# The first tile's modulation weights and first weights, laid out in memory in the order of their fetch

## The chip, the core and the metric

The kernel runs on one core of one Trainium2 chip. The metric is the device time of one execution in microseconds, as the median of several; three runs of the kernel before took 755.28 to 755.37, median 755.32. Five engines with their own instruction streams work side by side: TensorE (matrix products; PE, its weight loads PEld), VectorE (DVE), ScalarE (ACT), GpSimd (POOL) and SyncE (SP). In this kernel SP issues nearly all transfers from HBM, the chip's main memory, into the on-chip memory; sixteen DMA engines carry them out. An instruction waits until the transfer that it needs has landed on all of these.

## The reference

One decoder layer over 512 positions of width 1024 in fp32: two attention branches (forgetting and stick-breaking) fed by one input projection, a gated merge, a layer norm, a gated MLP with a short convolution, a second layer norm. Before each of the two sublayers a conditioning vector `c` scales and shifts the input:

```python
mod = c @ w_ada + b_ada
sh1, sc1, gt1, sh2, sc2, gt2 = [m[:, None, :] for m in jnp.split(mod, N_MOD, axis=-1)]
u = x * (1.0 + sc1) + sh1
proj = u @ w_in
```

So nothing of the projection can start before a part of `mod` is known: `sh1` and `sc1` for the rows of `w_in` that are to be used first. Each element of `mod` is an inner product of 1024 terms.

## The kernel before

**Tiles.** The width of 1024 is cut into eight tiles of 128 (`KT`), one channel to a partition. For tile `j` the kernel needs 128 rows of shift weights and 128 rows of scale weights (each row the 1024 weights of one element of `mod`), 128 rows of the input projection's first 904 columns with six bias values ahead of them (`w1`, 910 columns in all), and 128 rows of the transposed input (`xT`, 512 positions).

**Head.** At the start TensorE runs a few products with zeros (`zeros`), then four products that copy `c` to all partitions, a quarter of 256 columns into each of four PSUM banks (`grp[4]` to `grp[7]`), then more products with zeros. They don't use the modulation weights.

**Loading.** `first_load(j)` takes two tiles `wa` of 128x1024 (index 0 shift, index 1 scale), one `raw` for the first weights and one `xt`. For `j` above 0 these are four transfers. For `j` 0 they are cut finer: the weights come in halves of 512 columns, first half of shift, first half of scale, second half of shift, second half of scale, 256 KB each; then columns 0 to 389 of `w1`, then `xt`, then columns 390 to 909. All of these are issued by SP, in the order written (SP's order is set by hand). In HBM a row of `wa0` has 4096 bytes and one of `w1` 3640, so each of these cut transfers takes a part of every row. The transfers use eight completion semaphores in turn, so the ninth issue waits for the landing of the first.

**The first tile.** `first_zero` forms the inner products of tile 0, quarter by quarter as the broadcast of `c` is cut: for quarter `q` VectorE multiplies 256 columns of shift weights, then of scale weights, with `cq`, and sums along the row; the sum goes to `modr[:, w, 0, q]`, with `w` 0 for shift and 2 for scale. GpSimd adds up the partial sums of quarters 0 to 2, and the bias from the first columns of `raw`; VectorE adds the last quarter, which gives `modc`. ScalarE copies the quarters of `c` on for later use, splits the first 384 columns of the weights in two parts (`hi_of`; VectorE's `lo_of` makes the second), and applies scale and shift to `xt`, giving `uh`. Each fp32 product on TensorE is made of three products with such split operands. The block runs under `chain["on"]`, which keeps each engine's instructions in the order in which they are written.

**The tiles after it.** For `j` 1 to 7 `first_acc` makes the inner products with one VectorE instruction over 1024 columns each (line 216), `first_split` splits the weights, `first_mod` applies them, and `first_mm` adds 24 products per tile into eight banks (line 330). Two tiles are loaded ahead; five buffers stand for `wa`, four for `raw`. Where `chain` is off, the order on VectorE, ScalarE, GpSimd and TensorE is chosen by a planner with its own durations for instructions and transfers, within the dependencies and the orders given by hand (`issue_after`).

Lines of the profile: 227 to 230 are the loads of tile 0; 233 to 235 those of the others; 67 and 70 stand for every instruction recorded under `chain`; 100 and 103 are `hi_of` and `lo_of`.

Of the kernel before, what the change touches and what calls it, by code (L numbers as in the profile page):

```python
# [12 lines left out]
ALU = mybir.AluOpType  # L13
# [3 lines left out]
P = 128  # L17
T = 512
D = 1024
KT = D // P  # L20
# [8 lines left out]
W1B = W1C + 6  # L29
# [19 lines left out]
def layer_kernel(ctx: ExitStack, tc: tile.TileContext, out, xT, x, crow, wa0, wa1, w1, wct, wv, bf,  # L49
                 wp, wo, lncol, lnrow, wup, cwb, wdn):  # L50
    nc = tc.nc
# [23 lines left out]
    V, S, PE, G = Pinned(nc.vector), Pinned(nc.scalar), Pinned(nc.tensor), Pinned(nc.gpsimd)  # L75
# [54 lines left out]
    modr = const([P, 6, KT, 4], F32, "modr")  # L130
# [88 lines left out]
    def first_load(j):  # L219
        wa = [early.tile([P, D], F32, name=nm("wa"), tag="wa", bufs=5) for _ in range(2)]  # L220
        r = stg.tile([P, 1024], F32, name=nm("raw"), tag="raw", bufs=LOADS)
        xt = z(F32, "xt")
        if j == 0:
            for e in range(2):
                c = slice(e * 512, (e + 1) * 512)
                for q in range(2):
                    nc.sync.dma_start(wa[q][:, c], wa0[j, q][:, c])
            nc.sync.dma_start(r[:, 0:390], w1[j][:, 0:390])
            nc.sync.dma_start(xt, xT[j * P : (j + 1) * P, :])
            nc.sync.dma_start(r[:, 390:W1B], w1[j][:, 390:W1B])  # L230
        else:
            for q in range(2):
                nc.sync.dma_start(wa[q], wa0[j, q])
            nc.sync.dma_start(r[:, 0:W1B], w1[j])
            nc.sync.dma_start(xt, xT[j * P : (j + 1) * P, :])
        if j == 1:
            nc.sync.dma_start(bfs, bf)
        pend[j] = [wa, xt, r]
# [4 lines left out]
    def first_zero():  # L243
        wa, xt, r = pend[0]
        h, l = first_wide()
        for q in range(4):
            c = slice(q * 256, (q + 1) * 256)
            cq = grp[4 + q][:, 0:256]
            for w, t in zip((0, 2), wa):
                V.scalar_tensor_tensor(t[:, c], t[:, c], 1.0, cq, ALU.mult, ALU.mult, accum_out=modr[:, w, 0, q : q + 1])  # L250
            part = [modr[:, w, 0, :] for w in (0, 2)]
            if q == 0:
                G.tensor_scalar_add(part[1][:, 0:1], part[1][:, 0:1], 1.0)
            for w, m in zip((0, 2), part):
                if q in (1, 2):
                    G.tensor_tensor(m[:, 0:1], m[:, 0:1], m[:, q : q + 1], ALU.add)
                if q == 3:
                    V.tensor_tensor(modc[:, w, 0:1], m[:, 0:1], m[:, 3:4], ALU.add)
            for w, m in zip((0, 2), part):
                if q == 2:  # L260
                    G.tensor_tensor(m[:, 0:1], m[:, 0:1], r[:, w : w + 1], ALU.add)
            if q < 3:
                S.activation(cbc[:, c], cq, AF.Copy)
# [4 lines left out]
        r = r[:, 6:W1B]  # L268
# [501 lines left out]
    for p in (5, 6, 7):  # L770
        add_pair(p)
        for _ in range(3):
            if bj:
                j = bj.pop(0)
# [262 lines left out]
    for n in range(NSPLIT):  # L1037
        wt = weights(wui[n], 1 if n + 1 < NSPLIT else 0)
# [5 lines left out]
    for n in range(2 * FT):  # L1044
# [10 lines left out]
        t = z(F32, "cv")  # L1055
# [19 lines left out]
    for i in range(2):  # L1075
        t = fin.tile([P, D], F32, name=f"ln2_{i}", tag=f"ln2_{i}")
# [12 lines left out]
    for j in range(FT - LATE):  # L1089
        w = weights(wdi[j])  # L1090
# [4 lines left out]
    for i in range(NB):  # L1095
        tb = slice(i * P, (i + 1) * P)
        r = x1[i]
# [5 lines left out]
        for n, (e, c0, c1) in enumerate(pieces):  # L1103
            sole = (i, e) == own
            ps = bank()[:, 0 : c1 - c0] if sole else acc[i][e]
            for q in range(LATE):
                w = [ws[q][a][e][:, c0:c1] for a in range(2)]
# [19 lines left out]
def _pack(inputs):  # L1127
# [3 lines left out]
    c = np.ascontiguousarray  # L1131
    w_in, w_ada = a["w_in"], a["w_ada"]
    r = {}
# [1 line left out]
    r["x"] = a["x"][0]  # L1135
    r["crow"] = a["c"]
    wt = c(w_ada.T).reshape(6, KT, P, D)
    r["wa0"] = c(wt[0:2].transpose(1, 0, 2, 3))
    r["wa1"] = c(wt[2:6].reshape(4 * KT, P, D))
    bm = a["b_ada"].reshape(6, KT, P)  # L1140
    bcol = bm[[0, 3, 1, 4, 2, 5]].transpose(1, 2, 0).reshape(D, 6)
# [5 lines left out]

    first = [w_in[:, s : s + P] for s in (col("q", 0), col("k", 0), col("q", 1))]
    cols = np.concatenate([bcol] + first + [w_in[:, 2568:3080], w_in[:, 1536:1544]], axis=1)
    r["w1"] = c(cols.reshape(KT, P, W1B))  # L1150
    r["wv"] = c(w_in[:, 1024:1536].reshape(4, 2, P, 512).transpose(0, 2, 1, 3).reshape(4, P, D))
    starts = [col(*t) for t in TILES]
    r["wct"] = c(np.stack([w_in[:, s : s + P].reshape(KT, P, P).transpose(1, 0, 2).reshape(P, D) for s in starts]))
# [35 lines left out]
```

## Time and profile before

| | |
|---|---|
| median of three runs | 755.32 us (755.28 to 755.37) |
| the profiled execution's own time | 755.47 us |
| its span, first to last instruction | 753.3 us |
| TensorE busy | 741.5 us, 98% of the span |
| VectorE / ScalarE / GpSimd busy | 546.6 / 351.6 / 127.2 us |
| granted TensorE clock, mean | 0.998 |
| first product that uses loaded weights | 9.65 us |
| bytes moved | 100.46 MB, mean 133 GB/s |

A row of the timeline or of the chain of waits begins with the start in us and the duration in us, then the engine and the line; in brackets behind it stand the engine's idle time just before and what ended it. Rows of a group of instructions give a count (x4), busy time and mean. A row of the DMA issues gives what is written from what, the issuing engine's queue (SPq), how many issues, KB of each, and the median time from issue to landing. A row of windows gives, for a stretch of time, its length and then the busy time and count for PE, PEld, DVE, ACT and POOL, the granted clock, the DMA engines' share and GB/s.

### The profile page before, as it was taken

What the parts mean: (1) busy time and instruction counts of PE and PEld (TensorE: products, weight loads), DVE (VectorE), ACT (ScalarE), POOL (GpSimd) and SP (SyncE); (2) the same over time, 40 slices, a digit from 0 to 9 for tenths busy, and PEclk for the clock granted to TensorE, in tenths of its full rate; (3) what the DMA queues carried; (4) which work ended last, traced back from release to release, by engine and by line L of the source; (5) the groups of instructions that cost most, each with busy time, mean ns of one, the idle gap of its engine ahead of it and who ended that gap; (6) DMA issues with size and microseconds to landing.
All of it is one profiled execution on the core that took longest, in us unless ns stands there. A gap on an engine that the chain in (4) does not pass through costs nothing.

```text
span 753.3 us, 9519 instructions
## 1 busy us (share of the span) xinstructions
PE 741.5 (98%) x3502; PEld 620.8 (82%) x3502; DVE 546.6 (73%) x896; ACT 351.6 (47%) x587; POOL 127.2 (17%) x153
## 2 busy tenths in 40 slices
PE   8999999999999999999999999999999999999995
PEld 6878888888888888888898888888888888888885
DVE  6888989867688875596987887666755686333666
ACT  4568868368656654343246334444444442212300
POOL 3103000021110000000000690000000136455400
PEclk9999999999999999999999999999999999999999
DMA  8941332434334434564234424433333234324111
GB/s 328 405 164 56 113 120 105 141 99 153 103 114 136 154 112 167 169 232 164 86 112 140 157 98 137 134 118 125 127 115 109 85 110 150 103 85 140 56 40 73
DMA packets 31376, 100.46 MB, mean 133 GB/s; under 512 B 4145, under 2 KB 4673, under 8 KB 31330
## 3 DMA queue, kind: packets, MB, share of 16 engines
q1 hardware_dynamic: 29824, 97.69, 37.7%
q0 software_dynamic: 1504, 2.17, 1.1%
q8 instruction: 27, 0.44, 0.2%
q14 instruction: 19, 0.16, 0.1%
q10 hardware_dynamic: 2, 0.00, 0.0%
HBM read 96.63 MB, written 2.11 MB: 131 GB/s over the span
## 4 chain that ended last, share of the span: by engine, by line
PE 97%; DVE 1%; DMA 1%; ACT 0%; SPq 0%; issue 0%; DVEq 0%
PE ps L140 56%; PE ps L330 5%; PE ps L1085 5%; PE ps L1084 5%; PE ps L1086 5%; PE ps L613 3%; PE ps L70 2%; PE ps L585 2%; PE ps L794 2%; PE ps L796 2%; PE ps L795 2%; PE ps L523 1%; PE ps L522 1%; PE ps L496 1%; PE ps L497 1%; PE ps L498 1%
## 5 line engine op out<-in xcount | busy, mean ns | idle before, releaser
L103 DVE TENSOR_TENSOR wl<-raw,wh 128x1024 fp32r<-128x1024 f32 (+1 forms) x99 | 133.0, 1345 | 55.0 <-ACT wh L100 54.9
L140 PE MATMUL ps<-u2h,wh 128*128 128x512 f32 (+1 forms) x376 | 141.2, 376 | 0.0
L140 PE MATMUL ps<-u2l,wh 128*128 128x512 f32 (+1 forms) x376 | 141.0, 376 | 0.0
L140 PE MATMUL ps<-u2h,wl 128*128 128x512 f32 (+1 forms) x376 | 133.5, 375 | 0.0
L100 ACT ACTIVATE wh<-raw 128x1024 fp32r<-128x1024 f32 (+1 forms) x99 | 103.5, 1048 | 61.5 <-PE ps L1086 46.2
L140 PE MATMUL ps<-uh,wh 128*128 128x512 f32 x213 | 84.1, 395 | 0.0
L140 PE MATMUL ps<-ul,wh 128*128 128x512 f32 x213 | 83.3, 391 | 0.0
L140 PEld LDWEIGHTS ps<-u2h,wh 128*128 128x128 f32 x376 | 70.8, 188 | 13.0
L140 PEld LDWEIGHTS ps<-u2l,wh 128*128 128x128 f32 x376 | 70.8, 188 | 12.8
L140 PEld LDWEIGHTS ps<-u2h,wl 128*128 128x128 f32 x376 | 70.3, 188 | 12.6
L140 PE MATMUL ps<-uh,wl 128*128 128x512 f32 x213 | 78.9, 390 | 0.0
L683 POOL TENSOR_TENSOR raw<-raw,gt 128x1024 f32<-128x1024 f32 x22 | 56.4, 2568 | 92.8 <-DVE cv L1057 42.9
L1057 DVE SCALAR_TENSOR_TENSOR cv<-ps,cw,cv 128x511 f32<-128x511 f32 x44 | 32.9, 748 | 52.6 <-ACT cv L1056 52.6
L1056 ACT ACTIVATE cv<-ps,cw 128x512 f32<-128x512 f32 x44 | 34.1, 775 | 44.6 <-PE ps L140 44.6
L1084 PE MATMUL ps<-wh,hh 128*128 128x512 f32 x128 | 49.8, 389 | 0.0
L1085 PE MATMUL ps<-wl,hh 128*128 128x512 f32 x128 | 49.8, 389 | 0.0
L1086 PE MATMUL ps<-wh,hl 128*128 128x512 f32 x128 | 49.8, 389 | 0.0
L140 PEld LDWEIGHTS ps<-uh,wl 128*128 128x128 f32 x213 | 40.0, 188 | 8.7
L140 PEld LDWEIGHTS ps<-uh,wh 128*128 128x128 f32 x213 | 40.0, 188 | 8.0
L140 PEld LDWEIGHTS ps<-ul,wh 128*128 128x128 f32 x213 | 40.1, 188 | 7.8
L100 ACT ACTIVATE hh<-cv 128x512 fp32r<-128x512 f32 x22 | 13.9, 632 | 58.2 <-DVE cv L1064 58.2
L216 DVE SCALAR_TENSOR_TENSOR ada<-ada,cbc 128x1024 f32<-128x1024 f32 x24 | 29.2, 1218 | 8.7 <-DMA ada<-in_wa 8.6
(245 smaller groups left out, 1429.8 us busy)
## 6 DMA issues: line engine op xcount, KB each, us to landing
raw<-in_wup SPq DMA_DIRECT2D x44, 512.0 KB, 3.4
raw<-in_wct SPq DMA_DIRECT2D x29, 512.0 KB, 3.7
ada<-in_wa SPq DMA_DIRECT2D x24, 512.0 KB, 4.4
raw<-in_wdn SPq DMA_DIRECT2D x22, 512.0 KB, 3.3
wa<-in_wa SPq DMA_DIRECT2D x14, 512.0 KB, 7.4
raw<-in_wp SPq DMA_DIRECT2D x8, 512.0 KB, 3.3
raw<-in_wo SPq DMA_DIRECT2D x8, 512.0 KB, 3.4
raw<-in_wa SPq DMA_DIRECT2D x8, 512.0 KB, 3.3
```

The source lines that it names most:

```text
L100: S.activation(o, i, AF.Copy, scale=scale)
L103: return V.tensor_tensor(o, i, fl(hi), ALU.subtract)
L140: PE.matmul(ps, w, u, start=first and n == 0, stop=last and n == 2)
L216: V.scalar_tensor_tensor(wt, wt, 1.0, cbc, ALU.mult, ALU.mult, accum_out=raw)
L330: PE.matmul(grp[g], w, u, start=j == 0 and n == 0, stop=j == KT - 1 and n == (1 if g == 7 else 2))
L613: PE.matmul(ps[:, to : to + w], v_part(br, h, j), src[e][:, so : so + w], start=a == 0 and j == 0, stop=a == 1 and j == 3)
L683: G.tensor_tensor(r, r, gt[1], ALU.mult)
L1056: S.activation(t, ps, AF.Identity, bias=cw[:, n, 3:4], scale=cw[:, n, 2:3])
L1057: V.scalar_tensor_tensor(t[:, 1:], ps[:, 0:511], cw[:, n, 1:2], t[:, 1:], ALU.mult, ALU.add)
L1084: PE.matmul(ps, hh[j][:, tb], w[0], start=first, stop=False)
L1085: PE.matmul(ps, hh[j][:, tb], w[1], start=False, stop=False)
L1086: PE.matmul(ps, hl[j][:, tb], w[0], start=False, stop=last)
```

## The change

Three things change, all for tile 0 alone.

In the packing of the inputs on the host the two 512 KB blocks of `wa0[0]` are cut anew: the first block now holds, for each of the 128 rows, columns 0 to 511 of the shift weights and behind them columns 0 to 511 of the scale weights; the second block holds columns 512 to 1023 of both. `w1[0]` becomes flat: all rows' first 390 columns one after another, then all rows' remaining 520 columns.

In `first_load` two transfers of 512 KB, in rows of 4096 bytes, take the place of the four of 256 KB in rows of 2048; the two transfers of first weights read one contiguous stretch each, in rows of 1560 and 2080 bytes as before.

In `first_zero` the operand of each product is looked up in the new place: quarter `q` lies in `wa[q // 2]`, shift at 0 and scale at 512 columns, each with 256 columns for the quarter. The number of products, their sizes and their order stay.

```diff
         if j == 0:
-            for e in range(2):
-                c = slice(e * 512, (e + 1) * 512)
-                for q in range(2):
-                    nc.sync.dma_start(wa[q][:, c], wa0[j, q][:, c])
-            nc.sync.dma_start(r[:, 0:390], w1[j][:, 0:390])
+            flat = w1[j].rearrange("p c -> (p c)")
+            for q in range(2):
+                nc.sync.dma_start(wa[q], wa0[j, q])
+            nc.sync.dma_start(r[:, 0:390], flat[0 : P * 390].rearrange("(p c) -> p c", c=390))
             nc.sync.dma_start(xt, xT[j * P : (j + 1) * P, :])
-            nc.sync.dma_start(r[:, 390:W1B], w1[j][:, 390:W1B])
+            nc.sync.dma_start(r[:, 390:W1B], flat[P * 390 : P * W1B].rearrange("(p c) -> p c", c=W1B - 390))
...
-            for w, t in zip((0, 2), wa):
-                V.scalar_tensor_tensor(t[:, c], t[:, c], 1.0, cq, ALU.mult, ALU.mult, accum_out=modr[:, w, 0, q : q + 1])
+            for k, w in enumerate((0, 2)):
+                t = wa[q // 2][:, k * 512 + (q % 2) * 256 : k * 512 + (q % 2) * 256 + 256]
+                V.scalar_tensor_tensor(t, t, 1.0, cq, ALU.mult, ALU.mult, accum_out=modr[:, w, 0, q : q + 1])
...
-    r["wa0"] = c(wt[0:2].transpose(1, 0, 2, 3))
+    wa0 = c(wt[0:2].transpose(1, 0, 2, 3))
+    wa0[0] = wa0[0].reshape(2, P, 2, 512).transpose(2, 1, 0, 3).reshape(2, P, D)
+    r["wa0"] = wa0
...
-    r["w1"] = c(cols.reshape(KT, P, W1B))
+    w1 = c(cols.reshape(KT, P, W1B))
+    w1[0] = np.concatenate([w1[0, :, 0:390].ravel(), w1[0, :, 390:].ravel()]).reshape(P, W1B)
+    r["w1"] = w1
```

## The prediction

> **What bounds the kernel now.** First I read the busy shares and the shares of the chain of waits that ended last, from the profile's page.
>
> ```profile
> PE 741.5 (98%) x3502; PEld 620.8 (82%) x3502; DVE 546.6 (73%) x896; ACT 351.6 (47%) x587; POOL 127.2 (17%) x153
> PE 97%; DVE 1%; DMA 1%; ACT 0%; SPq 0%; issue 0%; DVEq 0%
> ```
>
> TensorE is busy nearly throughout, so what starts it late costs its full length. Where that start is late, the same chain in order of time (0 to 60 us) tells:
>
> ```profile
> 2.12 5.23 DMA wa<-in_wa
> 7.38 0.83 DVE wa L70 x5
> ...
> 8.59 0.17 DVE modc L70
> 8.79 0.82 ACT uh L70
> 9.65 41.15 PE ps L330 x179
> ```
>
> The only transfer in the chain is the fourth quarter of the first modulation weights. It is issued at 2.12, lands 5.23 later, at 7.35, and VectorE, ScalarE and TensorE follow in turn until the first real matmul at 9.65. From there to 50.80 the chain is TensorE alone, and the DMA's 1% of it is used up by these 5.23 us (0.7% of 753.3). So microseconds saved before 9.65 are kept as long as nothing new is late behind it.
>
> VectorE's rows of the head (timeline, 3.5 to 8.8) show who waits for which quarter:
>
> ```profile
> 3.56 0.42 DVE L67 SCALAR_TENSOR_TENSOR wa<-wa,ps 128x256 f32<-128x256 f32 x1 [1.09 <-PE ps L70]
> 4.95 0.42 DVE L70 SCALAR_TENSOR_TENSOR wa<-wa,ps 128x256 f32<-128x256 f32 x1 [0.96 <-DMA wa<-in_wa]
> ...
> 6.78 0.42 DVE L70 SCALAR_TENSOR_TENSOR wa<-wa,ps 128x256 f32<-128x256 f32 x1 [0.71 <-DMA wa<-in_wa]
> 7.38 0.42 DVE L70 SCALAR_TENSOR_TENSOR wa<-wa,ps 128x256 f32<-128x256 f32 x1 [0.17 <-DMA wa<-in_wa]
> 8.40 0.35 DVE L70 TENSOR_TENSOR modc<-modr 128x1 f32<-128x1 f32 x2
> ```
>
> Eight products (three and four stand in the gap), one every 0.34 us when nothing is missing: from 7.38 three of them to 8.40. The three waits that lie between them are all for transfers. After the last landing there are three products left, then the two additions that give `modc`.
>
> **The old transfers.** SP issues four of 256 KB, 0.47 apart; the view of DMA issues, asked for one issue at a time, gives 2.7, 3.7 and 5.0 us to landing for the first three:
>
> ```profile
> 0.73 1.82 SPq L227 DMA_DIRECT2D wa<-in_wa  x4
> wa<-in_wa SPq DMA_DIRECT2D x1, 256.0 KB, 2.7
> wa<-in_wa SPq DMA_DIRECT2D x1, 256.0 KB, 3.7
> wa<-in_wa SPq DMA_DIRECT2D x1, 256.0 KB, 5.0
> ```
>
> So the megabyte is in 6.62 us after its first issue (7.35 less 0.73). **The new transfers** are two of 512 KB with 4096-byte rows. This profile has such pairs on an idle queue, later in the kernel. Issue rows, then their times to landing (view of DMA issues over each single issue):
>
> ```profile
> 143.38 0.33 SPq L702 DMA_DIRECT2D ada<-in_wa  x1
> 143.75 0.90 SPq L154 DMA_DIRECT2D raw<-in_wct  x2
> ada<-in_wa SPq DMA_DIRECT2D x1, 512.0 KB, 3.3
> raw<-in_wct SPq DMA_DIRECT2D x1, 512.0 KB, 4.2
> 95.90 0.33 SPq L154 DMA_DIRECT2D raw<-in_wct  x1
> 96.50 0.33 SPq L154 DMA_DIRECT2D raw<-in_wv  x1
> raw<-in_wv SPq DMA_DIRECT2D x1, 512.0 KB, 4.4
> ```
>
> At 143 us the first lands 3.3 and the second 4.6 after the first issue (143.75 + 4.2 - 143.38); at 96 us the second lands 5.0 after it. A megabyte thus comes in 4.6 to 5.0 instead of 6.62. The old shape is slow elsewhere too: the rows of `x` in line 974 are 256 KB transfers that also take 2048 bytes out of 4096-byte rows; the fourth, issued at 349.33 in a burst that begins at 347.11, lands at 354.13, which is 7.0 after the burst's start.
>
> ```profile
> 347.11 0.33 SPq L974 DMA_DIRECT2D xn<-in_x  x1
> 349.33 0.38 SPq L974 DMA_DIRECT2D xn<-in_x  x1
> xn<-in_x SPq DMA_DIRECT2D x1, 256.0 KB, 4.8
> ```
>
> **The change, part by part.**
>
> (a) *Two issues fewer on SP.* Two times 0.47 is 0.94 us: everything queued behind, from the first weights (2.59 before) on, is issued at about 1.65. Nothing waits for the issue, since these transfers stand behind the modulation weights in the engines; I cost it at nothing. If that cover went, it could only help, by at most 0.94.
>
> (b) *The first half lands as 512 KB.* 0.73 + 3.3 = 4.03. Before, the first product ran at 3.56 (held by TensorE's broadcast of `c`), so it starts 0.5 later; the second, held until 4.95 before, now needs no wait. VectorE's floor is then 4.06 + 8 x 0.342 = 6.80 for the start of the `modc` additions.
>
> (c) *The second half* lands at 0.73 + 4.6 to 5.0 = 5.33 to 5.73. Behind it stand four products instead of three: start of the additions = landing + 0.03 + 4 x 0.342 = landing + 1.40, so 6.73 to 7.13, but not under 6.80. The old start was 8.40. The pairs' issues are 0.37 and 0.60 apart, the new ones 0.47, so I take a landing between the two, 5.5, and 6.90: **gain 1.50 us**.
>
> The far bound of (c) comes from packets on a queue in full flow: a stretch of 2048-byte rows (421 to 422) and one of 4096-byte rows (8.8 to 9.8), counts and share of 16 engines:
>
> ```profile
> DMA packets 80, 0.13 MB, mean 131 GB/s; under 512 B 16, under 2 KB 16, under 8 KB 80
> q1 hardware_dynamic: 80, 0.13, 34.5%
> DMA packets 112, 0.41 MB, mean 406 GB/s; under 512 B 13, under 2 KB 13, under 8 KB 112
> q1 hardware_dynamic: 112, 0.41, 99.1%
> ```
>
> 34.5% of 16 us over 64 large packets is 86 ns, 99.1% over 99 is 160 ns: twice the row saves 7% of the time for the same bytes. Each engine has eight rows of a transfer: 4 x 8 x 86 ns = 2.75 us against 2 x 8 x 160 = 2.56, so 0.19. If the rest of the old 6.62 belongs to the start of the execution and stays, the second half lands at 7.16. I take the pairs, since they are whole transfers from an idle queue like the new ones, and keep this end for the first rival.
>
> The Trainium skill ("DMA: Bandwidth & Descriptors", Why small descriptors are slow (HBM only)) gives each packet about 3 fixed cycles beside one for every 32 bytes: 2048-byte rows would lose 2.3% to 4096-byte rows, and the change would save some 0.06 us of 2.7, an estimate from that page. This speaks against the change; the packets in full flow are near it (7%), the pairs from an idle queue are not.
>
> (d) *POOL and ScalarE.* POOL adds partial sums and the bias that comes with the first weights, ScalarE splits these weights before it makes `uh`:
>
> ```profile
> 8.09 0.33 POOL L70 TENSOR_TENSOR modr<-modr,raw 128x1 f32<-128x1 f32 x2
> 8.12 0.52 ACT L70 ACTIVATE wh<-raw 128x384 fp32r<-128x384 f32 x1
> raw<-in_w SPq DMA_DIRECT2D x1, 195.0 KB, 5.3
> ```
>
> The 195 KB landed at 2.59 + 5.3 = 7.89, 0.54 behind the last quarter; with the same distance it is in by 5.9 to 6.3, before VectorE's fifth and sixth products let POOL go on. Its flat layout leaves its rows at 1560 and 2080 bytes; I give that no time, bounded by zero and the 0.54 itself, hidden behind products and sums as long as the landing stays under about 6.4.
>
> (e) *TensorE.* `uh` moves from 8.79 to 7.29 and the first matmul from 9.65 to 8.15. The warm-up matmuls end at 7.76 (5.52 + 2.24) and don't move, so they are just clear:
>
> ```profile
> 5.52 2.24 PE L70 MATMUL ps<-fpad 128*128 128x512 f32 x8
> ```
>
> (f) *What is late next.* The second tile:
>
> ```profile
> 12.95 0.96 ACT L100 ACTIVATE wh<-raw 128x904 fp32r<-128x904 f32 x1 [1.75 <-DMA raw<-in_w]
> 14.28 0.82 ACT L302 ACTIVATE uh<-xt,modc 128x512 fp32r<-128x512 f32 x1 [0.27 <-DVE modc L212]
> 15.14 0.30 PEld L330 LDWEIGHTS ps<-uh,wh 128*128 128x128 f32 x2 [0.39 <-ACT uh L302]
> ```
>
> ScalarE waits for the second tile's weights until 12.95, and its second `uh` at 14.28 is only 1.33 behind. For TensorE to keep 1.50 at 15.14, these weights must land 1.5 earlier. They stand behind the same bytes as before, so they follow the second half (7.35 to about 5.5, 1.85 earlier): 0.35 to spare. Behind it the chain is TensorE's own (41.15 us from 9.65).
>
> Sum: -1.50 (c) + 0 for (a), (b), (d), (e), (f). The profiled execution took 755.47 (span 753.3), 0.15 over the median of 755.32: 753.97 for such an execution, **753.8** for the median.
>
> **Rivals.**
>
> *The slow start is not the row length* (9%). Then (c) ends at its far bound: the second half lands at 7.16, the additions start at 8.56, 0.16 later than now, since four products stand behind it: 755.5. For it speak the packets in full flow, and that the old transfers lie in the first microseconds, for which this profile has no 4096-byte rows; against it the slow rows of `x` at 347 us and the pairs at 96 and 143.
>
> *A stalled pair* (5%, the slower side). The slowest pair of 4096-byte rows that I found:
>
> ```profile
> 230.64 0.33 SPq L154 DMA_DIRECT2D raw<-in_wct  x1
> ada<-in_wa SPq DMA_DIRECT2D x1, 512.0 KB, 6.5
> ```
>
> Its second was issued at 231.02 and landed at 237.52, 6.88 after the first issue. At the head: landing 7.61, additions at 9.01, 0.61 later than now, 755.9. It decides from a landing of 7.00 (8.40 - 1.40), because the first tile then has no quarter to work on meanwhile.
>
> *The second tile takes the place of the first* (14%). If stalls go on behind the second half, so that the second tile's weights gain only 0.7, TensorE gains 0.7 and waits the rest at 15.14: 754.6. In full this would undo the gain; the full rate behind 7.35 (next landing 0.54 later) speaks against it.
>
> *The planner* (6%). VectorE, ScalarE and POOL behind the head are ordered by a planner that reckons with transfers; another order could move either way, by about 1 us (TensorE's idle time behind 50.80 is 8.4 us in all, 702.50 less 694.07):
>
> ```profile
> 50.80:753.30 702.50, 694.07 (x3305) 582.32 (x3304) 506.27 (x803) 324.45 (x543) 117.54 (x121) 1.00 0.36 119
> ```
>
> **How the numbers follow.** The forecast has 66%, its own range 753.4 to 754.2: at best the floor with a first landing 0.2 earlier (gain 1.8 to 1.9), at worst the second half at 5.9. The range goes on to 755.5 to take in the second tile's case and half of the first rival's; what is left out is the stalled pair, half of the first rival, some of the planner and the last few per cent of the forecast's own. A change under 0.2% (1.51 us) can't be told from none here, and the forecast lies on that edge: a little over half of its share, with half of the planner's, is faster (0.40); the stalled pair in a worse form and some of the planner could be slower by that much (0.06); the rest is same (0.54).
>
> **What would show it.** Right: two landings near 4.0 and 5.5, a single long VectorE wait before the first product and at most a short one before the fifth, additions near 6.9, first matmul near 8.15, the second tile's weights before 11.4. Wrong: a second landing behind 7.0, a new TensorE wait at the second tile, or TensorE's idle time behind it other than 8.4 us.

## The result, and the profile after

The changed kernel takes 754.01 us (median of 22 runs, 753.58 to 755.16) against 755.28 us of the kernel before (22 runs, 754.75 to 755.59) on the same chip: 1.27 us less, a ratio of 0.9985 with a 95% interval of 0.9978 to 0.9992. The profiled execution took 753.64 (span 751.5), the one before 755.47 (753.3). The forecast was 753.8, and 753.97 for the profiled execution. The difference is real by its interval, and lies under the 0.2% (1.51 us) that had been named as the bound of "faster".

The shares of the page and of the chain of waits, kernel after:

```profile
PE 741.8 (99%) x3502; PEld 621.0 (83%) x3502; DVE 545.4 (73%) x896; ACT 351.9 (47%) x587; POOL 126.6 (17%) x153
PE 97%; DVE 2%; DMA 0%; ACT 0%; issue 0%; DVEq 0%
```

TensorE has the same work (741.8 us against 741.5) in a shorter span; the DMA has gone from 1% of the chain to 0%, and VectorE from 1% to 2%. Where, is told by the same chain in order of time, 0 to 60 us (start, duration, what):

```profile
0.73 3.35 DMA wa<-in_wa
...
4.20 0.43 DVE wa L67 x2
4.63 0.79 DVE wa L70 x5
...
5.57 1.17 DVE wa L70 x8
...
7.32 0.82 ACT uh L70
8.14 0.04 issue
8.19 41.16 PE ps L330 x179
```

The transfer in the chain is now the *first* half (issued 0.73, landed 4.09), not the last quarter. Behind it VectorE is never kept waiting. The timeline of the head (kernel after, up to 14 us) shows it:

```profile
4.20 0.42 DVE L67 SCALAR_TENSOR_TENSOR wa<-wa,ps 128x256 f32<-128x256 f32 x1 [1.73 <-DMA wa<-in_wa]
...
5.53 2.54 PE L70 MATMUL ps<-fpad 128*128 128x512 f32 x8
5.57 0.41 DVE L70 SCALAR_TENSOR_TENSOR wa<-wa,ps 128x256 f32<-128x256 f32 x1
...
6.94 0.35 DVE L70 TENSOR_TENSOR modc<-modr 128x1 f32<-128x1 f32 x2
...
11.57 0.96 ACT L100 ACTIVATE wh<-raw 128x904 fp32r<-128x904 f32 x1 [1.84 <-DMA raw<-in_w]
11.60 0.90 POOL L285 COPY bcols<-raw 128x6 f32<-128x6 f32 x1 [4.51 <-DMA raw<-in_w]
12.81 0.82 ACT L302 ACTIVATE uh<-xt,modc 128x512 fp32r<-128x512 f32 x1 [0.18 <-DVE modc L212]
13.68 0.53 PEld L330 LDWEIGHTS ps<-uh,wh 128*128 128x128 f32 x3 [0.36 <-ACT uh L302]
```

One wait of 1.73 before the first product, then eight products in a row: the fifth, which needs the second half, starts at 5.57 without a bracket, four times 0.342 behind the first. The second half had landed at 5.37 (by the last of the sixteen engines' completions in the trace, as for all landings here). The additions start at 6.94 against 8.40, the first real product on TensorE at 8.19 against 9.65. At the second tile TensorE waits 0.36 at 13.68 where it waited 0.39 at 15.14.

From the first real product to the last, each TensorE instruction is 1.43 to 1.48 us earlier than its twin of before, and the order on every engine is the same (SP has two issues fewer). TensorE's part behind 49.40 (a row of windows, with the columns of the one quoted for before):

```profile
49.40:751.50 702.10, 694.01 (x3305) 582.36 (x3303) 505.32 (x803) 324.58 (x543) 117.32 (x121) 1.00 0.35 119
```

Idle time is 702.10 - 694.01 = 8.09 us, against 8.43. The last matmul came only 1.47 earlier, while the span ended 1.83 earlier (751.49 against 753.32): the other 0.36 is the tail behind the landing of the last output (0.97 us against 1.33).

This tail is the change's too, by way of the two issues saved. When the work is done, SP waits for the eight completion semaphores in a fixed order, one every 0.06 us even when all have long been signalled (SP's own instructions at the end of the trace). Before, the last output, the 208th transfer that SP issues, had the first semaphore of that order, so all eight waits came behind its landing; now it is the 206th and has the seventh, so two do. The four profiled kernels with 208 issues (before, `e2`, `e3`, `e6`) all end 8.07 to 8.09 us behind their last matmul, the eight with 206 (after, `e1`, `e4`, `e5`, `e5c`, `e7`, `e9`, `e11`) 7.71 to 7.72; `e10` (205 issues, three waits behind the last landing) and `e13` (212, four) lie between, at 7.78 and 7.90. So the profiled pair differs by 1.47 from the head and 0.36 from the tail. The medians differ by less, 1.27: the profile before took 0.19 more than its kernel's median, the profile after 0.37 less than its own.

### The profile page after: what moved, and what is told of

It reads as the page before. It is cut to its first block, busy times and chain, and to the rows that moved or that the text cites. A ratio compares the mean times of both kernels' runs of the same rounds, so it can differ in the third digit from the quotient of the medians.

```text
span 751.5 us, 9515 instructions
## 1 busy us (share of the span) xinstructions
PE 741.8 (99%) x3502; PEld 621.0 (83%) x3502; DVE 545.4 (73%) x896; ACT 351.9 (47%) x587; POOL 126.6 (17%) x153
## 4 chain that ended last, share of the span: by engine, by line
PE 97%; DVE 2%; DMA 0%; ACT 0%; issue 0%; DVEq 0%
PE ps L140 56%; PE ps L330 5%; PE ps L1086 5%; PE ps L1084 5%; PE ps L1085 5%; PE ps L613 3%; PE ps L70 2%; PE ps L585 2%; PE ps L795 2%; PE ps L796 2%; PE ps L794 2%; PE ps L523 1%; PE ps L522 1%; PE ps L496 1%; PE ps L497 1%; PE ps L498 1%
```

## The experiments

Times are medians; "before" is the kernel before on the same chip. Landings, starts and shifts come from one profiled execution each.

### Which part of the change

`e1`, the modulation weights alone (the first weights laid out as before):

```diff
-            nc.sync.dma_start(r[:, 0:390], flat[0 : P * 390].rearrange("(p c) -> p c", c=390))
+            nc.sync.dma_start(r[:, 0:390], w1[j][:, 0:390])
...
-    w1[0] = np.concatenate([w1[0, :, 0:390].ravel(), w1[0, :, 390:].ravel()]).reshape(P, W1B)
```

> The new layout and the two transfers of the modulation weights, with the first weights (w1) laid out and read as in the kernel before. If the gain is all of the modulation weights: landings near 4.1 and 5.4, the modc additions at 6.9 to 7.0, first matmul near 8.2, second tile's weights near 11.6, time near 754.0. If the flat first weights carry a part of it: their first piece lands over 0.3 later than at 6.04, the additions or the second tile move by as much, time 754.3 or more.

`e2`, the first weights alone (the four transfers of modulation weights as before, the flat `w1[0]` as in the change):

```diff
-            nc.sync.dma_start(r[:, 0:390], w1[j][:, 0:390])
+            nc.sync.dma_start(r[:, 0:390], flat[0 : P * 390].rearrange("(p c) -> p c", c=390))
...
+    w1[0] = np.concatenate([w1[0, :, 0:390].ravel(), w1[0, :, 390:].ravel()]).reshape(P, W1B)
```

> Only the first weights are laid out flat; the modulation weights come as in the kernel before, four transfers of 2048 bytes out of each row of 4096. If the modulation weights carry the gain: fourth landing near 7.35, additions near 8.40, time near 755.3. If reading parts of rows of any pitch is what stalls the queue, the pieces behind 7.35 land a little closer together (under 0.5 us in all), still hidden.

Measured: `e1` 753.75 us against 755.19 (ratio 0.9984, 0.9975 to 0.9993); `e2` 755.09 against the same 755.19 (1.000, 0.999 to 1.001). The gain is the modulation weights'; the flat first weights show none. (In `e1` their first piece landed at 6.35, 0.31 behind the 6.04 of the changed kernel, but the flat layout has it as late as 6.53 in `e11` and 6.92 in `e9`, and the additions did not wait for it.) In `e2` the quarters land at 3.35, 5.86, 6.53 and 7.47, and the additions start at 8.53.

`e1`'s profile holds a surprise, though. Its halves land as in the changed kernel (4.17, 5.42) and its additions start at 7.02, but the first real product waits for something else. Timeline, kernel `e1`:

```profile
5.52 3.23 PE L70 MATMUL ps<-fpad 128*128 128x512 f32 x8
8.59 0.85 PE L329 MATMUL ps<-uh,wh 128*128 128x512 f32 x3
```

The same eight warm-up products took 3.23 us here, 2.54 in the changed kernel, 2.24 before: TensorE ran at half pace until 7.72 (its matmuls 0.43 us apart, then 0.23). Its `uh` was ready at 8.22; with the usual 0.05 behind that, the product would have started at 8.27. The first real product was 1.06 earlier than before, not 1.46; 0.28 of the missing 0.40 is got back at the second tile, where TensorE waits less, and the last TensorE instruction is 1.34 earlier.

### What makes the transfers faster

Four kernels separate three things that the change does at once to these transfers: it reads contiguous memory, it uses two issues, and its rows are twice as long.

`e3`, the four transfers of before in their order, but each quarter contiguous in memory:

```diff
+    wa0[0] = wa0[0].reshape(2, P, 2, 512).transpose(2, 0, 1, 3).reshape(2, P, D)
...
+                part = wa0[j, e].rearrange("p c -> (p c)")
                 for q in range(2):
-                    nc.sync.dma_start(wa[q][:, c], wa0[j, q][:, c])
+                    nc.sync.dma_start(wa[q][:, c], part[q * P * 512 : (q + 1) * P * 512].rearrange("(p c) -> p c", c=512))
```

> The kernel before with its four transfers of 256 KB in its order, each quarter contiguous in memory; rows still 2048 bytes, four issues, first weights as before. Theory of the stride (reading half of every row is slow on a fresh queue): landings near 3.4, 4.1, 4.75, 5.4, additions near 6.5, time near 753.4. Theory of the row length or of the number of issues: fourth landing near 7.3, additions near 8.4, time near 755.3.

`e4`, before with each block uncut, in two issues: all shift weights, then all scale weights:

```diff
-            for e in range(2):
-                c = slice(e * 512, (e + 1) * 512)
-                for q in range(2):
-                    nc.sync.dma_start(wa[q][:, c], wa0[j, q][:, c])
+            for q in range(2):
+                nc.sync.dma_start(wa[q], wa0[j, q])
```

> The kernel before with two uncut transfers of 512 KB, all of shift and then all of scale, memory as before. Landings near 4.1 and 5.4 as with the change; but the second product needs scale, so seven products stand behind the second landing: additions near 5.4 + 0.03 + 7 x 0.342 = 7.8, first matmul near 9.1, gain 0.6, time near 754.7. If the order of the fetch were worth nothing, additions near 6.9 and 754.0.

`e5`, the change with the memory as it was before: two issues, each reading 2048 of every 4096 bytes:

```diff
-                nc.sync.dma_start(wa[q], wa0[j, q])
+                nc.sync.dma_start(wa[q].rearrange("p (k c) -> p k c", c=512), wa0[j].rearrange("k p c -> p k c")[:, :, q * 512 : (q + 1) * 512])
```

> The changed kernel (two issues of 512 KB, new order of the fetch, flat first weights), but the modulation weights lie in memory as in the kernel before: each issue reads 256 pieces of 2048 bytes, half of every row of 4096. The number of issues alone: second landing near 5.4, additions 6.9, time near 754.0. Row length and stride: second landing near 7.2, additions near 8.6 (four products behind it), time near 755.5. If issues are worth the 1.1 us that contiguous quarters left open: second landing near 6.3, 754.9.

`e5c`, two issues, contiguous memory, but rows of 2048 bytes:

```diff
-    wa0[0] = wa0[0].reshape(2, P, 2, 512).transpose(2, 1, 0, 3).reshape(2, P, D)
+    wa0[0] = wa0[0].reshape(2, P, 2, 512).transpose(2, 0, 1, 3).reshape(2, P, D)
...
-                nc.sync.dma_start(wa[q], wa0[j, q])
+                part = wa0[j, q].rearrange("p c -> (p c)").rearrange("(k p c) -> p k c", k=2, c=512)
+                nc.sync.dma_start(wa[q].rearrange("p (k c) -> p k c", c=512), part)
```

> As the changed kernel, two issues of 512 KB from contiguous memory, but each cut into 256 rows of 2048 bytes instead of 128 of 4096. If the row length makes the rest of the slowness: second landing near 6.5, additions near 7.9, time near 754.8. If the number of issues makes it: second landing near 5.4, additions near 6.9, time near 754.0.

Measured (the last column is the ratio to before, with its interval):

| kernel | issues | memory | rows, bytes | last landing | additions | median | ratio |
|---|---|---|---|---|---|---|---|
| before | 4 | half of each row | 2048 | 7.35 | 8.40 | 755.28 | |
| `e3` | 4 | contiguous | 2048 | 6.49 | 7.58 | 754.69 | 0.9992 (0.9983 to 1.0002) |
| `e5` | 2 | half of each row | 2048 | 6.33 | 7.83 | 754.53 | 0.9991 (0.9981 to 1.0000) |
| `e5c` | 2 | contiguous | 2048 | 5.38 | 6.95 | 754.04 | 0.9986 (0.9977 to 0.9996) |
| after | 2 | contiguous | 4096 | 5.37 | 6.94 | 754.01 | 0.9985 (0.9978 to 0.9992) |
| `e4` | 2 | contiguous, shift then scale | 4096 | 5.60 | 8.02 | 754.34 | 0.9987 (0.9978 to 0.9997) |

Row length shows no effect: `e5c` has twice the packets of the changed kernel and lands 0.01 later. Contiguous memory is worth 0.86 with four issues (7.35 to 6.49) and 0.95 with two (6.33 to 5.38); two issues instead of four are worth 1.02 on half rows (7.35 to 6.33) and 1.11 on contiguous memory (6.49 to 5.38). Each landing is that of one profile. The eight profiles with two contiguous issues land between 5.27 and 5.76, the two with four contiguous issues at 6.49 and 6.18 (`e6`, below), the two with four issues of half rows at 7.35 and 7.47 (`e2`); half rows in two issues were profiled once. So both effects stand clear of the spread, but their sizes are known to some 0.3 us only. In the table the medians follow the order of the landings; part of the step between four issues and two is the tail of 0.36, which the kernels with two issues save whatever their landing.

The rate of arrival shows where these microseconds lie. Rows of windows, 1 us each from 2.50 on; the last two numbers are the share of the DMA engines and GB/s. Before (half rows, four issues):

```profile
2.50:3.50 1.00, 1.00 (x4) 0.81 (x3) 0.00 (x0) 0.26 (x2) 0.85 (x3) 1.00 1.20 256
3.50:4.50 1.00, 1.00 (x4) 0.81 (x3) 0.43 (x2) 0.00 (x0) 0.00 (x0) 1.00 0.56 182
4.50:5.50 1.00, 1.00 (x4) 0.72 (x4) 0.55 (x3) 0.09 (x1) 0.03 (x1) 1.00 0.85 257
```

`e3` (contiguous, four issues):

```profile
2.50:3.50 1.00, 1.00 (x4) 0.82 (x4) 0.00 (x0) 0.26 (x2) 0.85 (x3) 1.00 0.99 361
3.50:4.50 1.00, 1.00 (x4) 0.82 (x3) 0.82 (x4) 0.00 (x0) 0.00 (x0) 1.00 0.87 248
```

`e5` (half rows, two issues):

```profile
2.50:3.50 1.00, 1.00 (x4) 0.82 (x4) 0.00 (x0) 0.26 (x2) 0.85 (x3) 1.00 0.87 252
3.50:4.50 1.00, 1.00 (x4) 0.82 (x3) 0.00 (x0) 0.00 (x0) 0.00 (x0) 1.00 0.99 342
4.50:5.50 1.00, 1.00 (x4) 0.73 (x4) 0.40 (x3) 0.00 (x0) 0.00 (x0) 1.00 1.00 385
```

`e5c` (contiguous, two issues, short rows), then the kernel after:

```profile
2.50:3.50 1.00, 1.00 (x4) 0.82 (x3) 0.00 (x0) 0.27 (x2) 0.85 (x3) 1.00 1.04 401
3.50:4.50 1.00, 1.00 (x4) 0.82 (x3) 0.29 (x1) 0.00 (x0) 0.00 (x0) 1.00 1.04 406
```

```profile
2.50:3.50 1.00, 1.00 (x4) 0.82 (x4) 0.00 (x0) 0.26 (x2) 0.85 (x3) 1.00 0.99 393
3.50:4.50 1.00, 1.00 (x4) 0.82 (x3) 0.30 (x1) 0.00 (x0) 0.00 (x0) 1.00 1.02 414
```

With contiguous memory and two issues some 400 GB/s flow from 2.50 on. Half rows start at 252 and reach 385 only behind 4.50, with the same two issues; four issues on contiguous memory start at 361 and then drop to 248. Before had both. The start of the execution is thus not slow in itself.

Why either costs time is not shown, but the packets of the megabyte narrow it down. The median packet of 2048 bytes took 84 ns in all of these kernels; what differs is how many take far longer. With two issues, 29 of 512 packets took over 300 ns on half rows (`e5`, 12.5 us in the sum over the sixteen engines) and 3 on contiguous memory (`e5c`, 1.0 us). With four issues the count does not part the layouts: 20 and 11 on half rows (before, `e2`), 20 and 5 on contiguous memory (`e3`, `e6`). And the sixteen engines finish apart: the last piece before lands on the first engine at 5.46, on the middle ones at 6.20 and on the last at 7.35; after, at 5.00, 5.12 and 5.37. So of the 1.98 us between the two last landings 1.08 is common to the engines and the rest is that a few no longer lag.

`e4` tells what the order of the bytes adds. Its two transfers land as fast as after's (4.32, 5.60), but all scale weights come last, so seven products stand behind the second landing: 5.60 + 0.03 + 7 x 0.342 = 8.02, as measured. Landing faster gained 0.38 of the 1.46 there (8.40 to 8.02). With `e4`'s own landings and the cut by columns, the eight products would run from 4.43 to 7.17, so the cut is worth 0.85 of the rest; the other 0.23 is that this execution's first half came later than after's. Its median gained 0.85; its TensorE gained 0.53 in the profile and the tail 0.36, which accounts for it.

In `e3` the second tile takes a part of the gain. Timeline, kernel `e3`:

```profile
12.55 0.96 ACT L100 ACTIVATE wh<-raw 128x904 fp32r<-128x904 f32 x1 [2.02 <-DMA raw<-in_w]
14.47 0.53 PEld L331 LDWEIGHTS ps<-uh,wh 128*128 128x128 f32 x3 [0.52 <-ACT uh L303]
```

Its first product is 0.82 earlier (8.83), but the second tile's weights only 0.40 (12.55 against 12.95), and TensorE's wait there grows to 0.52: 0.67 are left at 14.47 (0.75 at TensorE's last instruction). Point (f) below says why 0.15 was lost and not the whole 0.42.

### Finer cuts

`e6`, four contiguous transfers of 256 KB in the order of the products (shift and scale of 256 columns each):

```diff
-                nc.sync.dma_start(wa[q], wa0[j, q])
+                part = wa0[j, q // 2].rearrange("p c -> (p c)")[(q % 2) * P * 512 : (q % 2 + 1) * P * 512]
+                nc.sync.dma_start(wa[q // 2][:, (q % 2) * 512 : (q % 2 + 1) * 512], part.rearrange("(p c) -> p c", c=512))
```

> The changed kernel with the modulation weights in four contiguous pieces of 256 KB (rows of 2048 bytes), a quarter of shift and scale together each, in the order of the products: the same transfers as with the contiguous quarters, but only two products stand behind the last. If four issues are slow again: landings near 3.4, 4.1, 5.6, 6.5, additions near 7.2, the second tile's weights near 12.5 and TensorE bound by them, time 754.5 to 754.7. If that was chance: fourth landing near 5.4, additions near 6.7, second tile's weights near 11.6, time 753.7 to 753.9, a little under the changed kernel's.

`e13`, the same with eight transfers of 128 KB, one for each product:

```diff
-            for q in range(2):
-                nc.sync.dma_start(wa[q], wa0[j, q])
+            for n in range(8):
+                part = wa0[j, n // 4].rearrange("p c -> (p c)")[(n % 4) * P * 256 : (n % 4 + 1) * P * 256]
+                nc.sync.dma_start(wa[n // 4][:, (n % 4) * 256 : (n % 4 + 1) * 256], part.rearrange("(p c) -> p c", c=256))
```

> The changed kernel with the modulation weights in eight contiguous pieces of 128 KB (rows of 1024 bytes), one for each product, in the order of the products. If each issue more costs (0.5 to 0.7 us from two to four): the eighth lands at 6.5 to 7.5 and the second tile's weights behind 12.5, time 754.7 or more. If the number of issues is worth nothing once the memory is contiguous: the eighth near 5.4, additions near 6.6, first matmul near 7.9, time 753.4 to 753.7.

Measured: `e6` 754.61 us against 755.33 (0.9994, 0.9985 to 1.0003); landings 3.50, 4.26, 5.40, 6.18, additions at 7.05, first product at 8.31. The first product of VectorE starts earlier (3.61), but the last quarter comes 0.81 later than in the changed kernel: a second look at four issues, with 6.18 beside the 6.49 of `e3`. No better than the change.

`e13` is slower: 756.07 us against 755.28 (1.0011, 1.0001 to 1.0020). Its timeline:

```profile
0.73 3.71 SPq L227 DMA_DIRECT2D wa<-in_wa  x8
4.49 0.43 SPq L228 DMA_DIRECT2D raw<-in_w  x1
...
8.92 0.30 DVE L70 TENSOR_TENSOR modc<-modr 128x1 f32<-128x1 f32 x2 [1.81 <-POOL modr L70]
14.85 0.96 ACT L100 ACTIVATE wh<-raw 128x904 fp32r<-128x904 f32 x1 [3.00 <-DMA raw<-in_w]
```

SP issues one transfer every 0.47 us, and the last six of the eight land 0.46 to 0.72 apart (up to 6.66). The first weights are issued at 4.49 and land at 8.56; POOL needs their bias, so the additions wait for it until 8.92 though the products were done, and the second tile's weights come at 14.82. The last TensorE instruction is 1.52 later than before.

### The cover of the first weights

`e10`, the change with the first weights of tile 0 in one transfer, `xt` behind it:

```diff
-            nc.sync.dma_start(r[:, 0:390], flat[0 : P * 390].rearrange("(p c) -> p c", c=390))
+            nc.sync.dma_start(r[:, 0:W1B], w1[j])
             nc.sync.dma_start(xt, xT[j * P : (j + 1) * P, :])
-            nc.sync.dma_start(r[:, 390:W1B], flat[P * 390 : P * W1B].rearrange("(p c) -> p c", c=W1B - 390))
```

> As the changed kernel, but the first tile's first weights come in one transfer of 455 KB (rows of 3640 bytes) ahead of xt, in place of two with xt between them: one issue fewer. If the number of issues is what costs: all 455 KB in near 6.7, xt near 7.3, second tile's weights up to 0.3 earlier, the additions unmoved near 6.9, time 753.7 to 754.0, and a narrower spread of the runs. If the first piece was needed early: the additions wait for the bias, near 7.2 to 7.4, time near 754.3.

Measured: 754.65 us against 755.28 (0.999, 0.9981 to 0.9998). The issues and a row of the timeline, kernel `e10`:

```profile
raw<-in_w SPq DMA_DIRECT2D x1, 455.0 KB, 6.1
...
8.10 0.30 DVE L70 TENSOR_TENSOR modc<-modr 128x1 f32<-128x1 f32 x2 [1.15 <-POOL modr L70]
```

The halves land as early as with the change (4.01, 5.27), but 455 KB are in only at 7.74, the additions wait 1.15 for POOL's sum with the bias, and the first product comes at 9.37. The cut of the first weights is needed, whatever their layout (754.65 here, 754.25 for the changed kernel on the same chip, `e11` below).

### The warm-ups, and the change again

`e7`, the change with four warm-up products in place of eight:

```diff
-WARM = 8
+WARM = 4
```

> The changed kernel with four products with zeros behind the broadcast of c instead of eight. In the profile with the modulation weights alone these products went on to 8.6 at the half clock and held the first real product (8.59 against 8.19). If they hold it in a part of the runs: median 0.05 to 0.2 under that of the changed kernel, its slowest runs nearer the median. If TensorE then loses its clock in the gap: first products at half speed, time 754.5 or more. If they never matter: the same as the changed kernel.

Measured: 754.27 us against 755.29 (0.9992, 0.9982 to 1.0001); six runs at 753.74 to 754.33, four at 755.3 to 756.75. The profiled execution took 755.7. Timeline of its TensorE:

```profile
6.31 2.27 PE L70 MATMUL ps<-fpad 128*128 128x512 f32 x4
8.85 1.65 PE L330 MATMUL ps<-uh,wh 128*128 128x512 f32 x3 [0.27 <-ACT uh L70]
...
12.94 0.86 PE L330 MATMUL ps<-ul,wh 128*128 128x512 f32 x3
```

TensorE ran dry for 0.27 us before its first real product, and then three of them took 1.65 us instead of 0.98 (kernel after: 8.19 to 9.17): it went on at half pace until 12.54, and three take 0.86 only from there on. From 8.85 to 12.54 at half pace costs some 1.7 us (3.69 x (1 - 0.23/0.43), by the distances of 0.43 and 0.23 between matmuls), most of the 2.1 by which this execution is above the changed kernel's. `c` also came late here (its broadcast started at 3.12, not 2.47), which moved the whole head. Fewer warm-ups are sometimes as good, and in this execution went with a whole spell at half pace; whether the other three executions above 755.2 had the same was not profiled.

`e11`, the changed kernel itself once more, without an edit, for the spread:

> The changed kernel once more, beside the others on the same chip. Median 753.8 to 754.2; its profile shows how far the landings vary between executions: second half 5.3 to 5.5, the transfers behind it by up to 0.9.

Measured: 754.25 us (11 runs, 753.55 to 754.99) against 755.28 (0.9986, 0.9977 to 0.9995). Its profiled execution took 754.5, with a head unlike the other one's. Timeline, kernel `e11`:

```profile
3.16 3.75 PE L70 MATMUL ps<-cbr,ones 97*128 97x256 f32 x8 [0.49 <-POOL fpad L195]
6.35 2.64 PE L70 MATMUL ps<-fpad 128*128 128x512 f32 x8
7.63 0.35 DVE L70 TENSOR_TENSOR modc<-modr 128x1 f32<-128x1 f32 x2
8.88 0.97 PE L330 MATMUL ps<-uh,wh 128*128 128x512 f32 x3
```

The halves land at 4.26 and 5.76, but TensorE's broadcast of `c` starts at 3.16 instead of 2.47, since the 4 KB of `c` came late (their packet took 1.03 us instead of 0.25; the row's bracket names GpSimd, which ended at about the same time, but in the kernel after the broadcast ran before GpSimd had done this). VectorE's products then wait for the broadcast, the additions for VectorE, and the first real product for `uh`, ready at 8.83. TensorE's first product is 0.77 earlier than before, its last instruction 0.60. The kernel before has the same broadcast and the same warm-ups, but its products waited for weights longer than that; the change has taken this slack away. The medians gain 1.27 and 1.03 us where the first pair of profiles shows 1.83 (1.47 and the tail's 0.36). Executions like this one, like `e9`'s (below) or like `e1`'s are the likely reason: in the five profiles with the change's head (after, `e5c`, `e1`, `e9`, `e11`) TensorE's last instruction is 1.47, 1.47, 1.34, 1.20 and 0.60 earlier than before. How often each occurs was not counted.

### The rows of `x`

`e9`, the change with the halves of `x` at line 974 laid out contiguously, 2048-byte rows as before (one run):

```diff
-            nc.sync.dma_start(xn[e], x[tb, e * 512 : (e + 1) * 512])
+            nc.sync.dma_start(xn[e], x[tb, :].rearrange("p c -> (p c)")[e * P * 512 : (e + 1) * P * 512].rearrange("(p c) -> p c", c=512))
```

> The changed kernel with the eight transfers of x ahead of the first layer norm (256 KB, 2048 bytes of each row of 4096, issued from an idle queue) read from contiguous halves. In the kernel before the fourth landed 7.0 us after the first issue. If the stride of half rows is the cause of the slow burst: 5.5 to 6. If the row length is: 6.5 to 7. The time of the kernel stays within 0.3 of 754.0, since TensorE has work there.

Measured: 753.89 us. The fourth of these transfers lands 6.7 us after the burst's start, against 7.04 before and 7.38 after. Median over six issues of that burst, kernel after, then `e9`:

```profile
xn<-in_x SPq DMA_DIRECT2D x6, 256.0 KB, 4.0
```

```profile
xn<-in_x SPq DMA_DIRECT2D x6, 256.0 KB, 3.6
```

The gain of 0.35 to 0.7 is smaller than the stride at the head would give (5.5 to 6 was expected), and the two profiles with strided rows differ by 0.34 among themselves. Part of what made these rows slow is their stride at most. Nor does it part the long packets here: 26 and 29 of the burst's 1024 took over 300 ns with half rows (before, after), 35 with contiguous halves.

The head of this execution shows a cover that failed. Timeline, kernel `e9`:

```profile
7.05 0.33 POOL L70 TENSOR_TENSOR modr<-modr,raw 128x1 f32<-128x1 f32 x2 [0.51 <-DMA raw<-in_w]
7.28 0.30 DVE L70 TENSOR_TENSOR modc<-modr 128x1 f32<-128x1 f32 x2 [0.39 <-POOL modr L70]
```

The first weights came at 6.92 (6.04 in the changed kernel's first profile), and both POOL and the additions waited for them; the first product started at 8.53.

## Why the prediction was right, point by point

The sum came out in the first profile: -1.50 forecast, -1.47 on TensorE. That the median came so near the 753.8 is in part luck: its 1.27 contain the tail's 0.36, which was in no term. If every execution has that tail, as the twelve profiles with 206 and 208 issues do, the head is worth some 0.9 us in the median (1.27 - 0.36, an estimate), since not every execution has the head of the first profile. The terms:

(a) *Two issues fewer cost nothing.* Right for the head: the first weights are issued at 1.64 (1.65 forecast), and nothing waits for it. But the step saw only SP's own time there. The number of issues also governs how fast the bytes come (0.8 to 1.1 us between four and two), with eight of them SP's interval of 0.47 decides (`e13`, slower), and at the end of the kernel the two issues fewer are worth the 0.36 of the tail, which no term of the sum had.

(b) *First half at 4.03, floor 6.80.* It landed at 4.09, and the first product started 0.11 behind it, where the step had put 0.03: 4.20 + 8 x 0.342 = 6.94.

(c) *Second half at 5.5, additions at 6.90.* It landed at 5.37, in the lower part of the 5.33 to 5.73 that the pairs at 96 and 143 us had given; with the step's 1.40 that allows 6.77. So the price was right to 0.04 us, but with some luck and by the other bound: not the second half but the floor of (b) sets the additions. The second half could land up to 5.54 (5.57 less 0.03) for nothing.

The reason given for choosing the pairs was only half right. The prediction took the old shape, 2048 out of 4096 bytes, as slow, and this shape is slow; but it makes only about half of the gap (0.86 to 0.95 of the 1.98 us), and the rest is the number of issues, which the prediction did not price. The pairs gave the right number, and they have both, contiguous blocks and two issues. Row length, which the change's own words name, is worth 0.01 us. The Trainium skill ("DMA: Bandwidth & Descriptors", Why small descriptors are slow (HBM only)), from which the prediction had estimated some 0.06 us for it, agrees with this comparison; it was no evidence against the change, as the prediction had put it, since the change did more than lengthen rows.

(d) *POOL and ScalarE hidden.* In the first profile: 195 KB landed at 6.04 (5.9 to 6.3 forecast). The limit of "about 6.4" was the right thing to name: `e9` at 6.92 and `e10` at 7.74 are past it, and the additions wait.

(e) *Warm-ups end at 7.76, don't move.* This step failed as it was put. They ended at 8.07 (5.53 + 2.54) in the first profile, 0.12 ahead of the first product, and at 8.75 in `e1`, where they hold it back by some 0.3. What was missed is that their length is not fixed: it depends on when TensorE leaves half pace, and their start on when `c` arrives. In `e11` it is the late `c` itself that costs: the broadcast had held the first product before (3.56), and the step put no price on its coming later.

(f) *The second tile's weights, 1.85 earlier, 0.35 to spare.* They landed at 11.55 against 12.93, 1.38 earlier; ScalarE's row moves from 12.95 to 11.57. This is 0.47 less than forecast. A reason that the landings suggest: 7.35 was the last of sixteen engines, and most were through earlier (6.20 for the middle ones) and could go on to the next bytes, so what stands behind gains less than the last landing does. This is argued, not tested.

By the step's own condition (1.5 earlier) it should have cost about 0.1. It didn't: the wait at the second tile is 0.36 against 0.39 before. The condition was too strict, and the step's own row shows it: before its second `uh` at 14.28 ScalarE sat idle for 0.27, waiting for `modc`. So the weights had 0.27 to spare, and 1.47 - 0.27 = 1.20 earlier was enough. Of the spare 1.47 - 1.38 = 0.09 was used, and 0.18 is left, as the bracket of the row at 12.81 says. In `e3` the head came 0.82 earlier and the weights 0.40; beyond the spare that leaves 0.15, and 0.15 was lost (0.67 at 14.47).

The second tile's `modc` moved with the head, because VectorE's two products for it stand right behind its work for the first tile. Rows of the timeline, before and then after:

```profile
12.70 1.22 DVE L216 SCALAR_TENSOR_TENSOR wa<-wa,cbc 128x1024 f32<-128x1024 f32 x1
12.98 1.00 POOL L285 COPY bcols<-raw 128x6 f32<-128x6 f32 x1 [4.42 <-DMA raw<-in_w]
14.01 0.16 DVE L211 TENSOR_TENSOR modc<-modr,bcols 128x1 f32<-128x1 f32 x1
```

```profile
11.23 1.22 DVE L216 SCALAR_TENSOR_TENSOR wa<-wa,cbc 128x1024 f32<-128x1024 f32 x1
12.54 0.16 DVE L211 TENSOR_TENSOR modc<-modr,bcols 128x1 f32<-128x1 f32 x1
```

The second product starts 1.47 earlier and `modc` 1.47 earlier. `modc` also waits for GpSimd's copy of the biases, but that copy's 1.00 and 0.90 us are not its own: it ends 0.05 to 0.06 behind VectorE's product in both (13.98 after 13.92, 12.51 after 12.45), and at the first tile it takes 0.20.

*Rivals.* "The slow start is not the row length" was right in its first words and wrong in its price: row length is nothing, but the start isn't slow (393 GB/s from 2.50 on), and the 5.37 excludes its 7.16. The stalled pair was seen in none of these profiles at the head; the latest second half of two contiguous issues landed at 5.76. The second tile as the next bound did not come in the changed kernel, but in `e3`, where 0.15 of 0.82 was lost to it. The planner changed no order.

*What would show it.* All held (4.09 and 5.37, one wait, 6.94, 8.19) except two: the second tile's weights came at 11.55, not before 11.4, and the idle time behind is 8.09, not 8.4, which the prediction had named as a sign of being wrong; it comes from the tail and not from TensorE's waits.

## What to carry to other kernels

Where a kernel's start hangs on a first load, give it contiguous blocks in as few issues as the consumer can bear, cut in the order of use: here contiguity and two issues instead of four were worth about 1 us each of landing, row length nothing, and the order of the bytes about 0.9 us on top. Once the first half's landing plus the consumer's own work sets the time, look at what stood behind the old wait (a broadcast, warm-ups of uncertain length, the next load), because that slack is gone. When the number of transfers changes, look at the kernel's end too: here which semaphore the last output happens to get was worth 0.36 us. To price a transfer, take one of the profile that is like it in contiguity and in number of issues, not in size and row length alone.

## What the runs showed of the hardware

*Half pace until an uncertain moment.* TensorE's matmuls of 512 columns follow each other 0.43 us apart at first and 0.23 later. The moment of change, read from these distances, was between 4.91 (`e2`) and 7.94 us (`e5`) in thirteen profiles with eight warm-ups, spread over the whole of it (5.64 before, 6.32 after), and 12.54 in `e7`, where TensorE had a gap of 0.27 at 8.58. The column of the granted clock stands at 1.00 in these stretches all the same (as in the rows of windows above), so here the row's own durations have to be read. The Trainium skill ("TensorE: Matmul & The Clock Gate", What's actually happening) has TensorE start throttled and released by activity, in a free-running window of 3413 ns that does not begin with the kernel. By that rule the change should come one to two windows behind the first matmul at 1.45, between 4.86 and 8.28 us (an estimate from that page's figure). All thirteen moments lie inside, so the traces agree with the window; the ±500 ns that the same section gives for the moment is narrower than the 3.03 us measured. `e7` is 4.6 us behind the last of them, more than one such window; a window counted back from 12.54 begins behind its gap and the one before holds the gap, but how a gap counts is not settled by one execution.

*A 4 KB transfer that takes 0.2 or 1 us.* The packet of `c` took 0.16 to 0.25 us in eleven profiles, but 1.01 to 1.08 in `e4`, `e7` and `e11`, where the broadcast starts at 3.12 to 3.20 instead of 2.47. In the same three SP's issue of the first weights took 1.12 to 1.19 us instead of 0.42, so more was held up than this packet. No kernel here changed this transfer, so the cause is open.

*A shift that keeps.* 1.46 us won at 8 us are 1.47 at 750: TensorE's waits behind the head moved along without loss.

*GpSimd's copy ends when VectorE's product does.* The copy of 128x6 biases takes 0.20 us at the first tile (6.89 to 7.09) and 0.90 at the second (11.60 to 12.51), where one of VectorE's products over 1024 columns is running; it ends 0.05 to 0.06 behind the end of such a product in all the profiles but `e13`, where it starts as the product ends and takes 0.20. In `e4`, `e10` and `e11` that is the first of the two products, and `modc` then starts 1.14 to 1.15 behind the second product's start; in the others it is the second, and `modc` starts 1.30 to 1.31 behind (1.45 in `e13`). No experiment tested this.
